# Attention scores in two matmul passes: the low part of the keys gets a zero-padded 128-row tile per head

## The chip, the cores and the metric

The kernel runs on one core of a Trainium2 chip. Five engines work side by side, each through its own queue in order: TensorE (matmuls; PE in the profile, its weight loads are shown apart as PEld), VectorE (DVE), ScalarE (ACT), GpSimd (POOL) and SyncE (SP), which issues the DMA transfers. The metric is the time of one execution on the device, in microseconds; lower is better.

## The reference, cut to what matters

The program is a two-layer block with three branches (mLSTM, sparse attention, retention) and a feed-forward part, for 512 tokens of width 1024. The change touches the attention branch alone. Its logits are, for 8 heads of width 64:

```python
q = (c_q @ a_wuq).reshape(b, s, A_HEADS, A_HEAD_DIM)
q_lat = einsum('bshd,hdc->bshc', q, a_wuk) * A_HEAD_DIM ** -0.5
logits = einsum('bthc,btkc->bthk', q_lat, kv_sel)
logits = where(valid, logits + bias, -inf)
probs = softmax(logits, axis=-1)
out = einsum('bthk,btkc->bthc', probs, kv_sel)
```

The 128 keys of a query are chosen by an indexer beforehand; the kernel keeps all keys and adds a mask instead. It moves `a_wuk` to the other side of the product: it computes a key of 64 numbers for each head and token from `c_kv`, and multiplies the query of 64 numbers with that.

## The kernel before

**Precision.** Large products are made of two parts per operand: a high part, which is the value rounded to the matmul's type by a copy, and a low part, which is the difference (`split`, lines 301 to 303: the copy on ScalarE, the subtraction on VectorE). A product is then three matmuls (`mm3`, lines 249 to 253): high by high, high by low, low by high.

**The score product.** A head is only 64 wide, and a matmul contracts over up to 128 rows of its operands. So `q_pair` (line 592) stores the query of a head twice in one 128-row tile: the high part in 64 rows, the low part in the other 64 (even heads have the high part in rows 0 to 63, odd heads in rows 64 to 127). `prepare` (line 671) makes the keys for a pair of heads: the tile `kk` of a head has the high part of its key in both halves. The first pass of line 707, `qs` by `kk` over 128 rows, is therefore (high + low query) by high key. What is left is high query by low key. The low parts of both heads of a pair lie in one tile, `kl`, the even head's in rows 0 to 63 and the odd head's in rows 64 to 127; the second pass of line 707 takes the 64 rows of a head from `qs` and from `kl`. Both passes add up in one PSUM tile.

**Units.** A unit (line 699) is one head and one block of 128 queries, 8 x 4 = 32 per layer. It makes the two score passes over 256, 256, 384 or 512 keys, adds bias and mask (`cmb`, GpSimd, line 709), adds that to the scores and takes the maximum (`prob`, `amx`, VectorE, line 712), exponentiates (ScalarE, line 715), transposes the probabilities (TensorE, line 721), copies them (ScalarE, line 723) and multiplies with the values (line 728). After a head's last block ScalarE scales the four results (`ha`, line 734).

**Order.** The units are generators. `wave_lazy` advances all that are under way by one step for each new one, and `tick` feeds them into the projections of the other branches (lines 558 to 565), one step for every two feature blocks or token blocks of a weight chunk. So a few short attention matmuls stand between runs of 512-column projection matmuls (`mm3`, lines 251 to 253). The order of each engine is fixed when the program is built; an engine waits in place when its next instruction isn't ready.

**Buffers.** Most tiles of 512 columns come from one pool, tag `r`, with 28 buffers (`NR`, line 142) that are handed out in turn: a new tile's first write waits until the last reader of the tile that had its buffer is done. `kk`, `kl`, `qs`, `cmb`, `prob` and `probT` are all of that tag.

**A twin.** The indexer (lines 623 and 624) has a product of the same build: `qs` with high and low query as weights, twice, by the high and the low part of its keys, both over 128 rows.

Of the kernel before, what the change touches and what calls it, by code (L numbers as in the profile page):

```python
# [11 lines left out]
F32 = mybir.dt.float32  # L12
F32R = mybir.dt.float32r
# [75 lines left out]
def wave_lazy(gens):  # L89
    active = []  # L90
    for g in gens:
        active.append(g)
        for x in list(active):
            if next(x, active) is active:
                active.remove(x)
        yield
    while active:
        for x in list(active):
            if next(x, active) is active:
                active.remove(x)  # L100
        yield


class Block:
# [546 lines left out]
    def attention(self, l, CT, masks, haT):  # L651
        nc, a = self.nc, self.a
        kv = [x[:, 3, :] for x in CT]
        V = [self.r(f"vv{s}") for s in range(NT)]
        with self.tc.high_priority():
            raw = self.wp.tile([128, 8, 64], F32, name="wuv", tag="raw", bufs=2)
            hi = self.wp.tile([128, 512], F32R, name="uvh", tag="whi")
            lo = self.wp.tile([128, 512], F32R, name="uvl", tag="wlo")
            nc.sync.dma_start(raw, a["a_wuv"][l].rearrange("h c d -> c h d"))
            self.split(hi, lo, raw.rearrange("p h d -> p (h d)"))  # L660
        for s in range(NT):
            p = self.sm()
            self.mm3(p, [x[:, s * 128:(s + 1) * 128] for x in kv], [hi, lo], True, True)
            nc.scalar.activation(V[s], p, AF.Copy)
            yield
        uk = self.r("uk", [4, 128])
        nc.sync.dma_start(uk, a["a_wuk"][l].rearrange("(f s) d c -> (s d) f c", s=2))
        ha = [self.r(f"ha{t}") for t in range(NT)]
        heads = {}

        def prepare(h):
            if h % 2 == 0:
                f = h // 2
                W = self.chunk(0, 2, [(0, a["a_wuq"][l][:, f * 128:(f + 1) * 128])], 128)
                p = self.sm()[:, 0:128]
                nc.tensor.transpose(p, uk[:, f, :], self.ident)
                ut = self.r("ut", [2, 128], F32R)
                self.split(ut[:, 0], ut[:, 1], p)
                qs = self.q_pair(W, 0, CT, 0.125, 0)
                yield  # L680
                p = self.sm()
                self.mm3(p, [ut[:, v] for v in range(2)], kv, True, True)
                kk = [self.r(f"kk{s}", dtype=F32R) for s in range(2)]
                lo = self.r("kl", dtype=F32R)
                for s in range(2):
                    x, y = (slice(0, 64), slice(64, 128))[::1 - 2 * s]
                    self.split(kk[s][x], lo[x], p[x])
                    nc.scalar.activation(kk[s][y], p[x], AF.Copy)
                heads["pair"] = qs, kk, lo
            qs, kk, lo = heads["pair"]  # L690
            tb = self.wk.tile([128, T], F32, name="tb", tag="tb", bufs=2)
            src = self.bias_dram[h, 0, 127:128]
            nc.sync.dma_start(tb, bass.AP(tensor=src.tensor, offset=src.offset, ap=[[639, 128], [1, T]]))
            s = h % 2
            x = slice(64 * s, 64 * s + 64)
            heads[h] = (qs[s], qs[s][x]), (kk[s], lo[x]), tb
            yield

        def unit(h, b):
            if b == 0:  # L700
                heads[h] += (self.sm([128, NT, 64]), self.stat(NT, "asum"))
            q, kk, tb, o, sums = heads[h]
            S = 128 * (b + 1)
            SP = max(S, 256)
            p = self.sm()[:, 0:SP]
            for v in range(2):
                nc.tensor.matmul(p, lhsT=q[v][:, b * 128:(b + 1) * 128], rhs=kk[v][:, 0:SP], start=v == 0, stop=v == 1)  # L707
            c = self.r("cmb", [S])
            nc.gpsimd.tensor_add(c, tb[:, T - S:T], masks[b] if b else self.neg)  # L709
            P = self.r("prob", [S])  # L710
            mx = self.stat(1, "amx")
            nc.vector.tensor_tensor_reduce(P, p[:, 0:S], c, 1.0, -3.0e38, op0=OP.add, op1=OP.max, accum_out=mx)  # L712
            nm = self.stat(1, "anm")
            nc.vector.tensor_scalar(nm, mx, -1.0, None, op0=OP.mult)
            nc.scalar.activation(P, P, AF.Exp, bias=nm, accum_out=sums[:, b:b + 1])
            yield
            yield
            yield
            pt = self.sm([128, 4, 128])
            for s in range(b + 1):  # L720
                nc.tensor.transpose(pt[:, s, :], P[:, s * 128:(s + 1) * 128], self.ident)  # L721
            PT = self.r("probT", [b + 1, 128])
            nc.scalar.activation(PT, pt[:, 0:b + 1], AF.Copy)
            yield
            yield
            yield
            for s in range(b + 1):
                nc.tensor.matmul(o[:, b, :], lhsT=PT[:, s, :], rhs=V[s][:, h * 64:(h + 1) * 64],  # L728
                                 start=s == 0, stop=s == b)
            if b == NT - 1:  # L730
                ri = self.stat(NT, "ari")
                nc.vector.reciprocal(ri, sums)
                for t in range(NT):
                    nc.scalar.activation(ha[t][:, h * 64:(h + 1) * 64], o[:, t, :], AF.Copy, scale=ri[:, t:t + 1])

        def units():
            yield prepare(0)
            yield iter(())
            for h in range(8):
                for b in range(NT):  # L740
                    if b == 2.0 and h < 7:
                        yield prepare(h + 1)
                    yield unit(h, b)

        yield from wave_lazy(units())
        for v, x in enumerate(self.branch_T("haT")):
            haT[v] = x
        for b in range(NT):
            self.to_T(ha[b].rearrange("p (f d) -> p f d", f=4), haT, b)
            yield  # L750
# [272 lines left out]
```

## Time and profile before

| | |
|---|---|
| median of 3 runs | 1861.61 us (1861.01 to 1861.81) |
| span of the profiled execution | 1862.3 us |
| TensorE busy | 1829.2 us (98%) |
| VectorE busy | 984.3 us (53%) |
| ScalarE busy | 734.4 us (39%) |
| GpSimd busy | 207.4 us (11%) |

The profiled execution is one execution; the median comes from others without the profiler, and the span counts from the first to the last instruction. A row of a timeline gives the start in us, the length in us, the engine, the line, the operation, what it writes and from what, and the form; `128*128 128x512` is a matmul that contracts over 128 rows into 128 rows of output, 512 columns wide, and `64*128` one over 64 rows. "xN" is a count, and a bracket at the end the idle time of the engine before it and what ended it. Matmuls overlap in their pipeline, so that a matmul's length is longer than its share of the engine: what a matmul costs is read from its start to the start of the next. A row of a table by stretch gives the stretch, its length, the busy time and the number of instructions of each engine in the order PE, PEld, DVE, ACT, POOL, then the granted clock of TensorE (1.00 is 2.4 GHz, 0.50 is 1.2 GHz), the busy share of the DMA engines and GB/s. In a group by line the numbers after the bar are the busy time in us, the mean in ns of one instruction, and the idle time before them with what ended it.

### The profile page before, as it was taken

To read this page: it belongs to the slowest core of one execution; us is meant where nothing else is said; L and a number is where in the kernel's file an instruction comes from. 1 tells how busy PE (TensorE), PEld (TensorE's weight loads), DVE (VectorE), ACT (ScalarE), POOL (GpSimd) and SP (SyncE) were. 2 spreads that over 40 slices of the span, in tenths; PEclk is the share of its full clock that TensorE was granted. 3 is DMA by queue.
4 is the path that set the end of the run, shared out by engine and by line. 5 is a ranking of instruction groups with operands and counts; after the bars stand their busy time and mean duration, and the time that the engine had idled before them with its cause. 6 is when DMAs were issued, how large, how long until landed. Compare 5 with 4: busy or idle time off the path is not lost.

```text
span 1862.3 us, 22844 instructions
## 1 busy us (share of the span) xinstructions
PE 1829.2 (98%) x8720; PEld 1504.7 (81%) x8720; DVE 984.3 (53%) x1798; ACT 734.4 (39%) x1202; POOL 207.4 (11%) x258
## 2 busy tenths in 40 slices
PE   9989999999999999999999899999999999999998
PEld 7868887777888888888888688877788898888886
DVE  5788985355455333332358899744545453333223
ACT  5552235555424323321245523355554343232221
POOL 3112240121000000000020132301210000000000
PEclk9989999999999999999999899999999999999999
DMA  5622323223234332323242223232222353323222
GB/s 183 204 79 74 111 72 100 79 71 97 80 136 136 102 100 92 102 91 102 100 128 80 62 80 102 66 105 82 72 74 95 109 164 97 101 92 102 91 99 82
DMA packets 126845, 185.95 MB, mean 100 GB/s; under 512 B 12256, under 2 KB 71136, under 8 KB 126736
## 3 DMA queue, kind: packets, MB, share of 16 engines
q1 hardware_dynamic: 125408, 178.98, 30.2%
q0 software_dynamic: 1184, 5.26, 0.8%
q8 instruction: 68, 1.11, 0.2%
q14 instruction: 41, 0.34, 0.1%
q10 hardware_dynamic: 144, 0.26, 0.1%
HBM read 177.64 MB, written 6.84 MB: 99 GB/s over the span
## 4 chain that ended last, share of the span: by engine, by line
PE 57%; DVE 8%; DMA 1%; issue 1%; ACT 1%; POOL 1%; SPq 0%; POOLq 0%; ACTq 0%; DVEq 0%
PE mm L251 18%; PE mm L253 18%; PE mm L252 17%; DVE wlo L234 2%; DVE mask L647 1%; PE sm L707 1%; DVE top L646 1%; PE sm L728 1%; DMA raw<-w_up 1%; PE sm L721 0%; POOL lnr L308 0%; ACT whi L233 0%; DVE ru L521 0%; DVE bst L356 0%; PE sm L345 0%
## 5 line engine op out<-in xcount | busy, mean ns | idle before, releaser
L234 DVE TENSOR_TENSOR wlo<-raw,whi 128x1024 fp32r<-128x1024 f32 (+2 forms) x302 | 371.7, 1232 | 598.0 <-ACT whi L233 597.5
L233 ACT ACTIVATE whi<-raw 128x1024 fp32r<-128x1024 f32 (+2 forms) x302 | 314.0, 1040 | 737.5 <-PE mm L252 303.6
L251 PE MATMUL mm<-hT,whi 128*128 128x512 f32 (+1 forms) x1216 | 469.3, 386 | 0.9 <-ACT fg L956 0.9
L252 PE MATMUL mm<-hT,whi 128*128 128x512 f32 (+1 forms) x1216 | 460.9, 379 | 1.0 <-DVE hT L303 1.0
L253 PE MATMUL mm<-hT,wlo 128*128 128x512 f32 (+1 forms) x1216 | 461.1, 379 | 0.0
L251 PEld LDWEIGHTS mm<-hT,whi 128*128 128x128 f32 x1216 | 228.8, 188 | 48.0 <-issue 4.6
L253 PEld LDWEIGHTS mm<-hT,wlo 128*128 128x128 f32 x1216 | 228.7, 188 | 44.0 <-issue 0.4
L252 PEld LDWEIGHTS mm<-hT,whi 128*128 128x128 f32 x1216 | 229.0, 188 | 42.1 <-DVE hT L303 1.6
L251 PE MATMUL mm<-whi,hT 128*128 128x512 f32 (+1 forms) x448 | 178.7, 400 | 1.7 <-ACT hT L302 1.7
L253 PE MATMUL mm<-whi,hT 128*128 128x512 f32 (+1 forms) x448 | 178.1, 398 | 0.0
L252 PE MATMUL mm<-wlo,hT 128*128 128x512 f32 (+1 forms) x448 | 177.4, 396 | 0.0
L253 PEld LDWEIGHTS mm<-whi,hT 128*128 128x128 f32 x448 | 86.0, 192 | 18.1 <-issue 0.9
L251 PEld LDWEIGHTS mm<-whi,hT 128*128 128x128 f32 x448 | 86.0, 192 | 17.6 <-ACT hT L302 2.1
L252 PEld LDWEIGHTS mm<-wlo,hT 128*128 128x128 f32 x448 | 86.1, 192 | 17.3 <-issue 1.3
L709 POOL TENSOR_TENSOR cmb<-tb,mask 128x256 f32<-128x256 f32 (+2 forms) x48 | 52.2, 1090 | 247.0 <-PE sm L721 78.7
L253 PE MATMUL mm<-whi,fa 128*128 128x512 f32 x192 | 75.6, 394 | 0.0
L251 PE MATMUL mm<-whi,fa 128*128 128x512 f32 x192 | 75.5, 393 | 0.0
L252 PE MATMUL mm<-wlo,fa 128*128 128x512 f32 x192 | 75.5, 393 | 0.0
L320 POOL TENSOR_SCALAR rs<-ms 128x1 f32<-128x1 f32 x16 | 5.7, 355 | 622.0 <-ACT hn L318 622.0
L712 DVE CUSTOM_DVE_ANT_0 prob<-sm,cmb 128x128 f32<-128x128 f32 (+1 forms) x64 | 31.1, 488 | 64.1 <-PE sm L707 63.4
L251 PE MATMUL mm<-whi,fr 128*128 128x512 f32 x160 | 62.4, 390 | 0.0
L253 PE MATMUL mm<-whi,fr 128*128 128x512 f32 x160 | 62.3, 389 | 0.0
(284 smaller groups left out, 2689.7 us busy)
## 6 DMA issues: line engine op xcount, KB each, us to landing
raw<-w_in SPq DMA_DIRECT2D x104, 512.0 KB, 3.5
raw<-w_gate SPq DMA_DIRECT2D x96, 256.0 KB, 2.8
raw<-w_up SPq DMA_DIRECT2D x96, 256.0 KB, 3.1
raw<-w_down SPq DMA_DIRECT2D x44, 512.0 KB, 3.6
raw<-w_out SPq DMA_DIRECT2D x16, 512.0 KB, 3.6
x<-x SPq DMA_DIRECT2D x8, 512.0 KB, 5.9
rot<-c_rot SPq DMA_DIRECT2D x16, 256.0 KB, 2.7
tb<-bias_dram SPq DMA_DIRECT2D x16, 256.0 KB, 3.4
```

Source lines behind the costliest of these rows:

```text
L233: nc.scalar.activation(h, r, AF.Copy)
L234: nc.vector.tensor_sub(o, r, h.bitcast(F32))
L251: t.matmul(out, lhsT=A[0], rhs=B[0], start=start, stop=False)
L252: t.matmul(out, lhsT=A[0], rhs=B[1], start=False, stop=False)
L253: t.matmul(out, lhsT=A[1], rhs=B[0], start=False, stop=stop)
L320: nc.gpsimd.tensor_scalar(r, ms[:, 0:1], ms[:, 1:2], EPS, op0=OP.add, op1=OP.add)
L646: nc.vector.max(m8, acc)
L647: nc.vector.match_replace(acc, m8, acc, TAKEN)
L707: nc.tensor.matmul(p, lhsT=q[v][:, b * 128:(b + 1) * 128], rhs=kk[v][:, 0:SP], start=v == 0, stop=v == 1)
L709: nc.gpsimd.tensor_add(c, tb[:, T - S:T], masks[b] if b else self.neg)
L712: nc.vector.tensor_tensor_reduce(P, p[:, 0:S], c, 1.0, -3.0e38, op0=OP.add, op1=OP.max, accum_out=mx)
L728: nc.tensor.matmul(o[:, b, :], lhsT=PT[:, s, :], rhs=V[s][:, h * 64:(h + 1) * 64], start=s == 0, stop=s == b)
```

## The change

Each head of a pair gets its own low tile, `kl0` and `kl1`, with the low part of its key in the rows in which its query has the high part. The other 64 rows are set to zero by a memset on GpSimd. The second pass takes all 128 rows of `qs` and of that tile; the rows in which the query has its low part meet the zeros.

```diff
--- before.py
+++ after.py
@@ -681,19 +681,19 @@
                 p = self.sm()
                 self.mm3(p, [ut[:, v] for v in range(2)], kv, True, True)
                 kk = [self.r(f"kk{s}", dtype=F32R) for s in range(2)]
-                lo = self.r("kl", dtype=F32R)
+                kl = [self.r(f"kl{s}", dtype=F32R) for s in range(2)]
                 for s in range(2):
                     x, y = (slice(0, 64), slice(64, 128))[::1 - 2 * s]
-                    self.split(kk[s][x], lo[x], p[x])
+                    nc.gpsimd.memset(kl[s][y].bitcast(F32), 0.0)
+                    self.split(kk[s][x], kl[s][x], p[x])
                     nc.scalar.activation(kk[s][y], p[x], AF.Copy)
-                heads["pair"] = qs, kk, lo
-            qs, kk, lo = heads["pair"]
+                heads["pair"] = qs, kk, kl
+            qs, kk, kl = heads["pair"]
             tb = self.wk.tile([128, T], F32, name="tb", tag="tb", bufs=2)
             src = self.bias_dram[h, 0, 127:128]
             nc.sync.dma_start(tb, bass.AP(tensor=src.tensor, offset=src.offset, ap=[[639, 128], [1, T]]))
             s = h % 2
-            x = slice(64 * s, 64 * s + 64)
-            heads[h] = (qs[s], qs[s][x]), (kk[s], lo[x]), tb
+            heads[h] = (qs[s], qs[s]), (kk[s], kl[s]), tb
             yield
 
         def unit(h, b):
```

The order of TensorE is the same row for row, but for the names and heights of these operands. Two things differ on other engines. In the rows below a bracket names the semaphores that an instruction waits for, by the engine or the DMA queue that raises them.

GpSimd, where the units of the fourth and fifth head stand (first layer; the names in it are `cmb`, bias plus mask of a unit, from `tb`, the bias, and a mask, and the `kl` tiles of the third pair). Before:

```order
L709 TENSOR_TENSOR cmb_3328<-tb_3199,mask1_434 128x256 [waits PE_49,Activation_49]
L709 TENSOR_TENSOR cmb_3433<-tb_3199,mask2_435 128x384 [waits DVE_49,PE_49,Activation_49]
L709 TENSOR_TENSOR cmb_3464<-tb_3199,mask3_436 128x512 [waits DMAHW1_49,PE_49]
L709 TENSOR_TENSOR cmb_3505<-tb_3428,cm_81 128x128 [waits DMAHW0_49,PE_49]
L709 TENSOR_TENSOR cmb_3535<-tb_3428,mask1_434 128x256 [waits DVE_49]
```

and in the changed kernel:

```order
L709 TENSOR_TENSOR cmb_3334<-tb_3205,mask1_434 128x256 [waits PE_49,Activation_49]
L687 MEMSET kl0_3427 64x512 [waits PE_49,Activation_49,Pool_49]
L687 MEMSET kl1_3428 64x512 [waits DVE_49,PE_49]
L709 TENSOR_TENSOR cmb_3442<-tb_3205,mask2_435 128x384 [waits PE_49,Pool_49]
L709 TENSOR_TENSOR cmb_3473<-tb_3205,mask3_436 128x512 [waits PE_49]
L709 TENSOR_TENSOR cmb_3514<-tb_3437,cm_81 128x128 [waits DMAHW0_49,DVE_49]
L709 TENSOR_TENSOR cmb_3544<-tb_3437,mask1_434 128x256 [waits PE_49,Activation_49]
```

Two memsets have come in ahead of the `cmb` of the fourth head's third block, and they wait for readers of the buffers that they get. All tiles after them get other buffers than before, so that the `cmb` of the fifth head's first block (`cmb_3505`, now `cmb_3514`) waits for VectorE instead of TensorE.

ScalarE, in the same place (`kk1` is the odd head's key tile of the third pair, `prob` the scores of the fourth head's third and fourth block, `anm` their negated maximum). Before:

```order
L723 ACTIVATE probT_3459<-sm_3456 128x256 [waits PE_49]
L688 ACTIVATE kk1_3420<-sm_3415 64x512 [waits DVE_49]
L715 ACT_TABLE_LOAD
L715 ACTIVATE prob_3435,asum_3288<-prob_3435,anm_3438 128x384 [waits DVE_49]
L715 ACTIVATE prob_3466,asum_3288<-prob_3466,anm_3469 128x512 [waits DVE_49,PE_49]
```

and in the changed kernel:

```order
L723 ACTIVATE probT_3468<-sm_3465 128x256 [waits PE_49]
L689 ACTIVATE kk1_3426<-sm_3421 64x512 [waits DVE_49]
L715 ACT_TABLE_LOAD [waits DVE_49]
L715 ACTIVATE prob_3444,asum_3294<-prob_3444,anm_3447 128x384 [waits Activation_49]
L715 ACTIVATE prob_3475,asum_3294<-prob_3475,anm_3478 128x512 [waits DVE_49,PE_49]
```

The load of the exponential's table stood free of waits; now it carries the wait for VectorE, and the exponential behind it, which waited for VectorE, waits for ScalarE's own earlier reader of a buffer.

## Rows read from the trace of the kernel before

**Rows 1.** Page, part 1: busy time, share of the span, instructions, TensorE alone

```profile
PE 1829.2 (98%) x8720; PEld 1504.7 (81%) x8720; DVE 984.3 (53%) x1798; ACT 734.4 (39%) x1202; POOL 207.4 (11%) x258
```

**Rows 2.** Table by stretch, first layer's attention stretch: busy time by engine

```profile
306.70:462.60 155.90, 154.77 (x737) 121.87 (x737) 74.91 (x170) 90.39 (x184) 27.05 (x27) 0.99 0.26 82
```

**Rows 3.** Line 707, its low pass: duration ns, starts, forms with counts

```profile
L707 PE MATMUL sm<-kl,qs x64: 379/410/502, 307.1 to 1383.8; 64*128 64x256 f32 x32, 64*128 64x384 f32 x16, 64*128 64x512 f32 x16
```

**Rows 4.** Timeline, 307.4 to 308.9: start us, length us, engine, line

```profile
307.49 0.19 PEld L707 LDWEIGHTS sm<-kk,qs 128*128 128x128 f32 x1
...
307.72 0.28 PE L707 MATMUL sm<-kk,qs 128*128 128x256 f32 x1
...
307.92 0.18 PEld L707 LDWEIGHTS sm<-kl,qs 64*128 64x128 f32 x1 [0.25 <-issue]
307.93 0.38 PE L707 MATMUL sm<-kl,qs 64*128 64x256 f32 x1
...
308.23 0.50 PE L251 MATMUL mm<-hT,whi 128*128 128x512 f32 x1
...
308.57 0.39 PE L252 MATMUL mm<-hT,whi 128*128 128x512 f32 x1
...
308.80 0.40 PE L253 MATMUL mm<-hT,wlo 128*128 128x512 f32 x1
```

**Rows 5.** Timeline of TensorE, the indexer's two 128-row passes

```profile
63.14 0.28 PE L623 MATMUL sm<-CT,qs 128*128 128x256 f32 x1
63.26 0.28 PE L624 MATMUL sm<-CT,qs 128*128 128x256 f32 x1
63.38 0.34 PE L623 MATMUL sm<-CT,qs 128*128 128x384 f32 x1
```

**Rows 6.** Timeline of TensorE, a 512-column score pair

```profile
343.68 0.40 PE L707 MATMUL sm<-kk,qs 128*128 128x512 f32 x1
344.00 0.50 PE L707 MATMUL sm<-kl,qs 64*128 64x512 f32 x1
344.43 0.39 PE L707 MATMUL sm<-kk,qs 128*128 128x256 f32 x1
```

**Rows 7.** Groups by line of GpSimd, the memset of that shape

```profile
L425 POOL MEMSET qz<- 64x512 f32 x8 | 4.2, 520 | 5.7 <-issue 5.4
```

**Rows 8.** Timeline, all engines, 386.0 to 392.6, fourth and fifth head

```profile
386.16 1.45 POOL L709 TENSOR_TENSOR cmb<-tb,cm 128x128 f32<-128x128 f32 x1
...
388.53 0.08 DVE L712 DVE_READ_ACCUMULATOR2_ANT amx<- 128x1 f32 x1
...
388.66 1.28 ACT L715 ACT_TABLE_LOAD   x1
...
389.13 0.15 DVE L714 TENSOR_SCALAR anm<-amx 128x1 f32<-128x1 f32 x1
...
389.80 0.29 DVE L712 CUSTOM_DVE_ANT_0 prob<-sm,cmb 128x128 f32<-128x128 f32 x1
...
389.96 0.62 ACT L715 ACTIVATE prob<-prob,anm 128x384 f32<-128x384 f32 x1
...
391.60 0.50 PE L721 MATMUL sm<-cm,prob 128*128 128x128 f32 x3
...
392.37 0.39 ACT L715 ACTIVATE prob<-prob,anm 128x128 f32<-128x128 f32 x1
```

**Rows 9.** Table by stretch, granted clock: third number from the right

```profile
138.20:377.00 238.80, 235.00 (x1205) 194.10 (x1203) 172.02 (x425) 100.73 (x179) 54.09 (x55) 1.00 0.29 88
377.04:380.45 3.41, 3.41 (x9) 2.71 (x9) 2.45 (x4) 3.37 (x6) 0.00 (x0) 0.50 0.28 105
1298.64:1302.05 3.41, 3.41 (x8) 2.66 (x9) 2.35 (x4) 3.37 (x6) 0.00 (x0) 0.50 0.24 91
```

**Rows 10.** Waits of TensorE: total us, times, longest us

```profile
PE sm L915 <- DVE rsc L900: 2.9, 2, 1.4
...
PE sm L707 <- ACT ha L734: 2.0, 2, 1.0
```

## Prediction

> **What bounds the kernel now.** I read the page's first part first: TensorE is busy for 98% of the span [rows 1]. That share alone proves little, because a matmul's row counts as busy until its modelled end, so I read starts instead of lengths from here on. The second view is the table of one stretch, the 156 us of the first layer in which the attention units are fed into the projections. TensorE is busy for 154.77 of 155.90 us there, ScalarE for 90.39, VectorE for 74.91, GpSimd for 27.05 [rows 2]. The second layer repeats it, up to its last low pass at 1383.8 [rows 3]. So in the place that the change touches TensorE sets the pace, and time taken out of its queue is time off the end, unless another engine's answer then comes too late.
>
> The third view is the group of the low pass: 64 matmuls of form 64*128, 32 of them 256 columns wide, 16 of 384 and 16 of 512 [rows 3]. The fourth is TensorE's timeline, read from start to start. A 512-column projection matmul starts 0.23 us before the next one (308.57 to 308.80). Around a low pass all three steps are longer [rows 4]. The high pass of 256 columns starts at 307.72, the low pass at 307.93 (0.21 later), the next projection matmul at 308.23 (0.30 later), and the one after it at 308.57 (0.34 instead of 0.23). The weight loads say why: the high pass's load starts at 307.49, 0.23 us ahead of its matmul, while the low pass's starts at 307.92, together with it. The matmul ahead of a 64-row one takes longer, the 64-row one has its load in the open, and so has the one behind it.
>
> **What the change takes away.** The kernel before has a twin of the new form: the indexer's two passes (lines 623 and 624), both over 128 rows, with the same weights loaded twice as in line 707. Their 256-column steps are 0.12 and 0.12 us (63.14, 63.26, 63.38) [rows 5]. So a 256-column pair with the step behind it takes 0.21 + 0.30 + 0.34 = 0.85 us now, and as 128-row matmuls 0.12 + 0.12 + 0.23 = 0.47: 0.38 us less. For 512 columns the pair starts at 343.68, the low pass at 344.00 and the next matmul at 344.43, thus 0.32 + 0.43 = 0.75 us against 2 x 0.23 = 0.46 [rows 6]; with the same 0.11 of the step behind, 0.40 less. I take 0.39 for 384 columns, which lies between. The sum is 32 x 0.38 + 16 x 0.39 + 16 x 0.40 = 24.8 us. Both row halves are in these 64, and TensorE's order is the same row for row in the changed kernel, so nothing is added on that engine.
>
> The Trainium skill has a rule for this ("TensorEngine Tiling (Array Packing)", Key Properties): changing the tiling mode drains the engine. The trace agrees in kind [rows 4]. With the 128 cycles that "TensorE: Matmul & The Clock Gate", Step-by-step: what each phase is for, gives for a drain, two per pair at 2.4 GHz are an estimate of 64 x 0.107 = 6.8 us, a quarter of what the steps show; the steps decide, since they hold the loads too.
>
> **What it adds.** Sixteen GpSimd memsets of 64 x 512, two per pair of heads, four pairs per layer. The same shape takes 0.52 us where the program has it already [rows 7], so 16 x 0.52 = 8.3 us of GpSimd, which is busy for 27 of 156 us there [rows 2]. They are not free by themselves: GpSimd works in order, a memset waits until the last reader of its buffer is done, and behind it stand the additions of bias and mask (cmb, line 709), for which VectorE's prob (line 712) waits. I went through the waits that the changed order names and set each releaser's end in the trace against the waiter. The second low tile also moves which buffer every later tile of the 28 gets. The closest case is the cmb of the fifth head's first block. It starts at 386.16 now and will wait for amx of an earlier unit, written until 388.61; its 1.45 us then end at 390.06, and the prob that reads it starts at 389.80 [rows 8]. That prob comes 0.3 us late, and VectorE's order now puts a gate multiply (line 493) ahead of it as well. What waits for it first is ScalarE's exponential, which starts at 392.37, 2.3 us after that prob ends at 390.09 [rows 8]; this cover hides it and I cost it at nothing. Were the cover gone, TensorE would lose the 0.3 us in each layer. The memsets themselves I also cost at nothing: their tiles are read a head later.
>
> **What comes late next.** TensorE gets ahead of answers that it waits for. The closest one in the order is ScalarE's table load ahead of the exponential of the fourth head's third block. It runs at 388.66 now, before VectorE's anm at 389.13 is there; in the changed order the load itself waits for anm, which ends at 389.28. So the exponential ends at 389.28 + 1.28 + 0.62 = 391.2 instead of 390.58, and its transposes (line 721) start at 391.60 now [rows 8]. Two score pairs stand on TensorE's way there, 0.78 us, so about 0.6 + 0.78 - 1.0 = 0.4 us is waited, in each layer. Other answers come close where short matmuls stand in a row; I allow 0.35 us more per layer, so 1.5 us in all. The bounds are nothing (no wait is removed, so no gain) and three places per layer that each lose two pairs' saving, 2 x 3 x 0.78 = 4.7 us. I take 1.5, near the one place that I can work out.
>
> The clock is the last term. TensorE's granted clock was 0.50 in 377.04 to 380.45 and in 1298.64 to 1302.05, behind the two idles of 1.0 us of line 707, and 1.00 from 138.20 to 377.00, though that stretch has one of the two idles of 1.4 us of line 915 [rows 9, 10]. So a short idle does not bring it down by itself; what lies around it decides. At 0.50, the 1.2 GHz level, 3.41 us hold 8 matmuls of 0.43 instead of 15 of 0.23, a loss of about 1.6 us each. In the changed kernel all of this comes some us earlier and closer together, so I take the more common outcome of such an idle, that both falls are gone: 3.2 us.
>
> **The sum.** The profiled execution's span is 1862.3 us: 1862.3 - 24.8 + 1.5 - 3.2 = 1835.8. The median of the runs before, 1861.6, is 0.7 below that span, so I forecast 1835.1 us.
>
> **The rivals.** (1) The gain comes as worked out, but the clock falls in these places again, or in others: 1835.1 + 3.2 = 1838.3 us. For it speaks that both layers fell at the same place. (2) TensorE gets ahead of softmax everywhere: score pass, prob, exponential and transposes of a unit hang together, and half of the saving turns into waits: 1862.3 - 12.4 - 0.7 = 1849.2. Against it stands ScalarE's share of 90 in 156 us [rows 2]. (3) The 128-row form gains nothing: a full-height load cannot start while a full-height matmul runs, both loads of a pair stay in the open, and the steps stay 0.21, 0.30, 0.34: 1861.6 us. Against it stand the load at 307.49, ahead of its matmul, and the twin's 0.12 [rows 4, 5]. The Trainium skill states it so ("TensorE: Matmul & The Clock Gate", The mechanism): a load overlaps a running matmul only where the row groups differ; the trace differs. (4) Slower: the memsets stand ahead of the cmb additions, and their buffers come free so late that VectorE, and then TensorE in its fixed order, waits once in each of the 8 pairs for a whole lead of cmb over prob, 389.80 - 386.16 = 3.64 us [rows 8]. It decides from the point where 8 such waits exceed 24.8 us, that is 3.1 us each; 8 x 3.64 = 29.1, so 1861.6 + 4.3 = 1865.9. Against it stands that the releasers found end a head before the use.
>
> **How the numbers follow.** Forecast 0.50, rival 1 0.28, rival 2 0.12, rival 3 0.03, rival 4 0.03, and 0.04 for a larger gain. A measurement of this kernel can tell some 0.2%, 3.7 us, from no change: forecast, rivals 1 and 2 and the larger gain are faster (0.94), rival 3 is the same (0.03), rival 4 slower (0.03). The range goes down to 1831.8 (no waits: 1833.6; one half-clock stretch fewer elsewhere: 1.6 more, plus the error of steps read to 0.01 us) and up to 1841.5 (rival 1 with the waits at their bound, 3.2 more). Beyond it lie rivals 2 to 4 and half of the 0.04, 0.20 together.
>
> **What would show it.** In the profile after, the second pass of line 707 (708 there) should have the form 128*128, its load should start about 0.2 us ahead of it, and the steps of a 256-column pair should be 0.12, 0.12, 0.23. The attention stretch should shrink by about 12 us in each layer, and everything before 306 us stay. Waits of TensorE for prob or cmb at that place would be rivals 2 or 4. Steps still at 0.30 would be rival 3 and the prediction's end. Granted clock of 0.50 inside the stretch would be rival 1.

## The result, and the profile after

| | before | after |
|---|---|---|
| median, same chip | 1861.31 us (1859.96 to 1861.81, 4 runs) | 1838.68 us (1837.55 to 1840.39, 4 runs) |
| span of the profiled execution | 1862.3 us | 1838.5 us |
| attention stretch, layer 1 / layer 2 | 166.5 / 166.7 us | 154.2 / 154.3 us |
| the rest, up to the end of TensorE's last matmul | 1521.5 us | 1522.6 us |

The ratio is 0.9888 with an interval of 0.9877 to 0.9899; the medians are 22.6 us apart. Of 1861.31 us the interval is 18.8 to 22.9 us, so a saving is known to some 2 us, and no closer. The forecast was 1835.1 us, range 1831.8 to 1841.5. The attention stretch is counted here from the first start of line 707 in a layer to the start of TensorE's 59th row behind the last one, on the same instructions in every kernel.

First the page of the kernel after, part 1, and a table by stretch (stretch, its length, busy time of PE, PEld, DVE, ACT, POOL, granted clock, DMA share, GB/s). They answer [rows 1, 2, 9].

```profile
PE 1803.9 (98%) x8720; PEld 1497.9 (81%) x8720; DVE 985.8 (54%) x1798; ACT 733.1 (40%) x1202; POOL 215.1 (12%) x274
...
306.40:460.90 154.50, 152.62 (x797) 128.28 (x797) 78.33 (x176) 93.99 (x194) 29.91 (x33) 1.00 0.29 88
1216.40:1370.90 154.50, 152.60 (x796) 128.13 (x796) 78.31 (x176) 93.83 (x194) 29.91 (x33) 1.00 0.28 84
```

TensorE is busy for 98% as before, with as many instructions; the busy share alone would not tell that anything had happened. The granted clock is 1.00 over both attention stretches, where one fall of 3.41 us made 0.99 of it in [rows 2]; the falls at 377 and 1298 us [rows 9] are not there. GpSimd has 16 instructions and 7.7 us more.

Next the group of the low pass (length ns least/median/most, first and last start, forms) and TensorE's timeline around one 256-column pair, as in [rows 3, 4].

```profile
L707 PE MATMUL sm<-kl,qs x64: 274/310/401, 306.8 to 1360.1; 128*128 128x256 f32 x32, 128*128 128x384 f32 x16, 128*128 128x512 f32 x16
```

```profile
306.92 0.40 PE L253 MATMUL mm<-hT,wlo 128*128 128x512 f32 x1
306.92 0.19 PEld L707 LDWEIGHTS sm<-kk,qs 128*128 128x128 f32 x1
307.15 0.28 PE L707 MATMUL sm<-kk,qs 128*128 128x256 f32 x1
307.16 0.19 PEld L707 LDWEIGHTS sm<-kl,qs 128*128 128x128 f32 x1
...
307.27 0.28 PE L707 MATMUL sm<-kl,qs 128*128 128x256 f32 x1
307.27 0.19 PEld L251 LDWEIGHTS mm<-hT,whi 128*128 128x128 f32 x1
307.39 0.40 PE L251 MATMUL mm<-hT,whi 128*128 128x512 f32 x1
307.39 0.19 PEld L252 LDWEIGHTS mm<-hT,whi 128*128 128x128 f32 x1
```

The pair starts at 307.15 and 307.27 and the projection matmul follows at 307.39: 0.12 and 0.12 us where [rows 4] had 0.21 and 0.30. The load of the low pass starts at 307.16, 0.11 ahead of its matmul; before it started with it. Medians of the steps in ns, each over the places where the neighbours on that side are projection matmuls and nothing waits:

| columns of the pair | step of the high pass | step of the low pass | step behind (512 columns) |
|---|---|---|---|
| 256 | 209 → 117 | 310 → 119 | 337 → 233 |
| 384 | 264 → 173 | 370 → 174 | 337 → 233 |
| 512 | 327 → 231 | 431 → 234 | 337 → 233 |

Most high passes stand behind a transpose (line 721) or a product with the values (line 728); their step is some 0.08 us longer in both kernels and falls by the same 88 to 96 ns. So a 64-row low pass cost 0.09 us ahead of it, 0.19 in itself (0.20 at 384 and 512 columns) and 0.10 behind.

### The profile page after: what moved, and what is told of

Same layout as the page of the kernel before. It is cut to its first block, busy times and chain, and to the rows that moved or that the text cites. A ratio compares the mean times of both kernels' runs of the same rounds, so it can differ in the third digit from the quotient of the medians.

```text
span 1838.5 us, 22889 instructions
## 1 busy us (share of the span) xinstructions
PE 1803.9 (98%) x8720; PEld 1497.9 (81%) x8720; DVE 985.8 (54%) x1798; ACT 733.1 (40%) x1202; POOL 215.1 (12%) x274
## 4 chain that ended last, share of the span: by engine, by line
PE 58%; DVE 7%; DMA 1%; ACT 1%; issue 1%; POOL 1%; SPq 0%; POOLq 0%; ACTq 0%; DVEq 0%
PE mm L253 18%; PE mm L251 18%; PE mm L252 18%; DVE wlo L234 2%; DVE mask L647 1%; DVE top L646 1%; PE sm L728 1%; DMA raw<-w_up 1%; PE sm L707 1%; ACT whi L233 1%; PE sm L721 0%; DVE ru L521 0%; PE sm L368 0%; POOL lnr L308 0%; PE sm L345 0%
## 5 line engine op out<-in xcount | busy, mean ns | idle before, releaser
L252 PE MATMUL mm<-wlo,fr 128*128 128x512 f32 x160 | 62.3, 389 | 0.0
```

The source lines that it names most:

```text
L252: t.matmul(out, lhsT=A[0], rhs=B[1], start=False, stop=False)
```

## What the experiments had to tell apart

The theory: the price belongs to the change of matmul height, 128 rows to 64 and back, and is paid on each visit; the zeros, memsets and other buffers are free or nearly so; what of the gain is missing went into a few waits on softmax. The rivals: the gain came by the other buffers or the clock and not by the height; each 64-row matmul is dear by itself; the memsets or the wait at the table load took a share back. Times of the kernel before that stand beside a run are from the same chip. That the zeros themselves make the second pass fast is not among the rivals: the twin of [rows 5] has the same step of 0.12 us with both halves full.

**The changed kernel once more.** It shows how much one execution differs from the next.

> The changed kernel again, beside the others on one chip. Both theories: 22 to 24 us under the kernel before, TensorE waiting 0.6 us per layer for the exponential at 384 us.

Measured: 1838.51 us (1838.21 to 1840.99) against 1860.23 for before, ratio 0.9881 (0.9868 to 0.9895). The stretches are 154.18 and 154.33 us. The rest is 2.2 us shorter than in the first profile, with 3.4 us less of half clock around 1034 us. So a stretch repeats within 0.1 us, and differences of 2 us in the rest of two profiles say nothing.

**All of the change but the height.** The two padded tiles, the memsets and the new buffers stay; the second pass takes 64 rows again.

```diff
-            heads[h] = (qs[s], qs[s]), (kk[s], kl[s]), tb
+            x = slice(64 * s, 64 * s + 64)
+            heads[h] = (qs[s], qs[s][x]), (kk[s], kl[s][x]), tb
```

> The changed kernel's tiles and memsets, but the low pass takes 64 rows again (the zeros are never read). Theory (the height of the matmul is what costs): steps back at 0.21, 0.30, 0.34 us, time within 2 us of the kernel before, so 1860 to 1863. Rival (two heads no longer share one low tile, and that is what frees TensorE): near 1839.

Measured: 1861.39 us against 1860.23, ratio 1.0006 (0.9997 to 1.0015). The group of the low pass (line 708 in this kernel) and TensorE's timeline:

```profile
L708 PE MATMUL sm<-kl,qs x64: 379/410/502, 308.0 to 1381.8; 64*128 64x256 f32 x32, 64*128 64x384 f32 x16, 64*128 64x512 f32 x16
```

```profile
308.62 0.28 PE L708 MATMUL sm<-kk,qs 128*128 128x256 f32 x1
308.83 0.38 PE L708 MATMUL sm<-kl,qs 64*128 64x256 f32 x1
309.14 0.50 PE L251 MATMUL mm<-hT,whi 128*128 128x512 f32 x1
309.47 0.40 PE L252 MATMUL mm<-hT,whi 128*128 128x512 f32 x1
```

The steps are 0.21, 0.31 and 0.33 again. The whole gain hangs on the height: the interval of the ratio leaves room for at most 0.6 us of it. The stretches are 166.65 us, with one fall of the clock in it, and 165.36 without: the memsets and the buffers cost nothing that shows, and a fall of 3.41 us at half clock costs some 1.3 us.

**Half of the heads.** Even heads with 128 rows, odd heads with the 64 rows that hold their key.

```diff
-            heads[h] = (qs[s], qs[s]), (kk[s], kl[s]), tb
+            x = slice(64, 128) if s else slice(0, 128)
+            heads[h] = (qs[s], qs[s][x]), (kk[s], kl[s][x]), tb
```

> Even heads take the low pass over 128 rows, odd heads over 64. Theory (a fixed price per low pass of 64 rows between matmuls of 128): half the steps fall, the two attention stretches shrink by about 6.2 us each, time about 11 to 12 us under the kernel before. Rival (the price is paid once per stretch or depends on which half of the rows): nearly all or nearly none of the gain.

Measured: 1848.48 us against 1859.31, ratio 0.9938 (0.9923 to 0.9953). The stretches are 159.07 and 159.42 us, about half way between 154.2 and the 165.4 of 64 rows without a fall. The price is one per low pass; it does not depend on what the other heads do.

**Two 64-row matmuls in a row.** In the kernel before, the low pass of 512 columns is cut into two of 256, with the same weights. A price per matmul would be paid twice, a price per change of height once.

```diff
-                nc.tensor.matmul(p, lhsT=q[v][:, b * 128:(b + 1) * 128], rhs=kk[v][:, 0:SP], start=v == 0, stop=v == 1)
+                for c0, c1 in ((0, 256), (256, 512)) if v and SP == 512 else ((0, SP),):
+                    nc.tensor.matmul(p[:, c0:c1], lhsT=q[v][:, b * 128:(b + 1) * 128], rhs=kk[v][:, c0:c1],
+                                     start=v == 0, stop=v == 1 and c1 == SP)
```

> The kernel before with the 512-column low pass cut into two 64-row matmuls of 256 columns with the same weights; 16 matmuls more. Theory A (the price is in the change of height): the step from the first half to the second is 0.12 us, that from the second to the next 0.30 as before. Theory B (every 64-row matmul has its load in the open): 0.30 for both halves, 0.18 x 16 = 3 us more in all.

Measured: 1859.94 us in one run, against 1859.31. TensorE and its weight loads at such a place; "x2" are the two halves in one row:

```profile
343.99 0.40 PE L708 MATMUL sm<-kk,qs 128*128 128x512 f32 x1
...
344.32 0.29 PEld L708 LDWEIGHTS sm<-kl,qs 64*128 64x128 f32 x2 [0.36 <-issue]
344.32 0.50 PE L708 MATMUL sm<-kl,qs 64*128 64x256 f32 x2
...
344.75 0.39 PE L708 MATMUL sm<-kk,qs 128*128 128x256 f32 x1
```

From the first half at 344.32 to the next pass at 344.75 it is 0.43 us, as for the uncut pass in [rows 6]. The medians of the two steps are 223 and 207 ns, 430 in all against 431, and the step behind is still 337. The expected split, 0.12 and 0.30, did not come. The first half's load starts 2 ns ahead of its matmul, the second's 116 ns ahead: it overlaps the first half, which takes the same 64 rows. So a visit of two 64-row matmuls pays once. How the sum splits tells more: against the 119 ns of 256 columns without a change, the first half has 0.10 more and the second 0.09. These are the price behind a change and the price ahead of one, so the 0.19 of a single low pass is the first change's second part and the second change's first part.

The same cut with 128 rows is the control.

> The same cut in the changed kernel, as a control: two 128-row halves of 256 columns. Both theories: 0.12 us for each half, no difference to the changed kernel in the sum.

Measured: 1838.54 us in one run; halves of 118 and 119 ns, 237 against 234 uncut. The cut itself is free.

**The low pass first.** In the kernel before, the 64-row pass goes ahead of the 128-row one.

```diff
-            for v in range(2):
-                nc.tensor.matmul(p, lhsT=q[v][:, b * 128:(b + 1) * 128], rhs=kk[v][:, 0:SP], start=v == 0, stop=v == 1)
+            for v in (1, 0):
+                nc.tensor.matmul(p, lhsT=q[v][:, b * 128:(b + 1) * 128], rhs=kk[v][:, 0:SP], start=v == 1, stop=v == 0)
```

> The kernel before with the two passes of line 707 in the other order, the 64-row low pass first. Theory (a change of height in the middle of 128-row matmuls has a price on both sides, whatever stands there): the low pass keeps its 0.30, 0.37 and 0.43 us, the step of the matmul behind it, now the high pass, is about 0.1 longer, and the step ahead of it too; the attention stretches as in the kernel before, 165 to 167 us. Rival (the price comes from two passes into one PSUM tile in this order): it changes by more than 3 us per stretch.

Measured: 1859.0 us in one run, against 1859.66. TensorE:

```profile
307.35 0.39 PE L253 MATMUL mm<-hT,wlo 128*128 128x512 f32 x1
307.67 0.38 PE L707 MATMUL sm<-kl,qs 64*128 64x256 f32 x1
307.98 0.38 PE L707 MATMUL sm<-kk,qs 128*128 128x256 f32 x1
308.20 0.40 PE L251 MATMUL mm<-hT,whi 128*128 128x512 f32 x1
```

Now the projection matmul ahead takes 0.32 instead of 0.23, the low pass 0.31, and the high pass behind it 0.22 instead of 0.12. The three parts of the price have moved with the 64-row matmul. The stretches are 164.50 us and, with one fall of the clock, 166.10. No order within the pair avoids it.

**The memsets away.** Three low tiles outside the pool, zeroed once; the pool has 26 buffers instead of 28 for the room.

```diff
-NB8, NR = 8, 28
+NB8, NR = 8, 26
...
-                kl = [self.r(f"kl{s}", dtype=F32R) for s in range(2)]
+                kl = [self.low[0], self.low[1 + f % 2]]
...
-                    nc.gpsimd.memset(kl[s][y].bitcast(F32), 0.0)
```

> The changed kernel without memsets in the loop: three low tiles stand outside the pool and are zeroed once in each half that stays zero, with 26 buffers of tag r (the same memory as 29). Theory (GpSimd's memsets are hidden): within 1 us of the run with 29 buffers, unless the other buffers bring waits of their own. Rival (the 16 memsets cost VectorE or TensorE something): 3 us or more under it.

Measured: 1839.62 us against 1860.23, ratio 0.9882 (0.9869 to 0.9896), the same as the changed kernel. The memsets were hidden. The stretches are 0.3 to 0.5 us shorter, and the wait of line 721 that comes below is not in this kernel's waits.

**One more buffer.** With 29 buffers the table load of the exponential stands free of its wait again.

```diff
-NB8, NR = 8, 28
+NB8, NR = 8, 29
```

> The changed kernel with 29 instead of 28 buffers of tag r. Theory (the waits that ate part of the gain come from the buffers having moved by one, which put a wait on ScalarE's table loads): the table loads stand free again, TensorE's waits at 384, 418 and 431 us go, 2 to 3 us per execution less than the changed kernel, about 25 to 26 us under the kernel before. Rival (TensorE now simply outruns softmax): the waits stay, within 1 us of the changed kernel.

Measured: 1838.49 us against 1860.23, ratio 0.9877 (0.9862 to 0.9892). The stretches are 153.25 and 153.46 us, 0.8 to 0.9 less per layer, and the wait of line 721 is gone. The load of the table, which waits for `anm` in the changed kernel, here follows the activation ahead of it without a wait:

```profile
385.24 0.59 ACT L689 ACTIVATE kk<-sm 64x512 fp32r<-64x512 f32 x1 [1.72 <-DVE kl L303]
385.86 1.28 ACT L715 ACT_TABLE_LOAD   x1
```

The median is that of the changed kernel, 21.7 us under the kernel before and not the 25 to 26 that were expected; an interval of some 2.8 us to either side could hardly show the 1.7 us of the stretches. In the profile there are waits elsewhere. TensorE's waits (total us, times, longest), and a table by stretch:

```profile
PE sm L915 <- DVE rsc L900: 3.5, 2, 2.9
...
PE mm L251 <- DVE sg L481: 2.2, 2, 1.1
```

```profile
252.93:256.34 3.41, 3.41 (x18) 3.41 (x17) 1.86 (x9) 0.60 (x1) 0.23 (x1) 0.50 0.34 88
```

Line 251 now waits for `sg`, 1.1 us in each layer, which is more than the stretch gained; the profiles of the changed kernel have no such wait. Line 915 waits once for 2.9, and 3.41 us at half clock stand behind that; this may belong to this execution alone, which was the longest of the four (1841.62). That the table load's wait came with the buffers is shown; that the wait for `sg` is what kept the median where it was is likely, but one profile does not show it.

**The same edit on other short matmuls.** The mLSTM's gate rows are products over 36 rows (lines 800 and 811, 12 matmuls). Here they are padded to 128 with zeros, on top of the change.

```diff
-        self.sel = self.const.tile([36, 4], F32R, name="sel")
+        self.sel = self.const.tile([128, 4], F32R, name="sel")
...
-        rows = [self.r("rows", parts=36, dtype=F32R) for _ in range(2)]
+        rows = [self.r("rows", dtype=F32R) for _ in range(2)]
...
```

> The changed kernel with the mLSTM's 12 matmuls of 36 rows (lines 800 and 811) padded to 128 rows in the same way, since their rows show steps of 0.33 us for 512 columns at full clock and up to 0.72 at half clock. Theory (a matmul of fewer rows costs the same here): the steps around them fall to 0.23 (0.43 at half clock); 1 to 3 us under the changed kernel unless TensorE's wait of 3.6 us for VectorE just ahead takes it up, then nothing. Rival (only 64-row forms cost): steps unchanged.

Measured: 1832.47 us against 1859.31, ratio 0.9852 (0.9836 to 0.9869), about 6 us below the changed kernel (1838.54 in the control on the same chip), more than expected. TensorE in the changed kernel, at half clock:

```profile
131.66 0.63 PE L252 MATMUL mm<-wlo,hT 128*128 128x512 f32 x1
132.21 0.79 PE L800 MATMUL sm<-rows,sel 36*128 36x512 f32 x1
132.94 0.79 PE L253 MATMUL mm<-whi,hT 128*128 128x512 f32 x1
133.53 0.63 PE L251 MATMUL mm<-whi,hT 128*128 128x512 f32 x1
```

and with 128 rows:

```profile
131.51 0.63 PE L252 MATMUL mm<-wlo,hT 128*128 128x512 f32 x1
131.94 0.63 PE L800 MATMUL sm<-rows,sel 128*128 128x512 f32 x1
132.36 0.63 PE L253 MATMUL mm<-whi,hT 128*128 128x512 f32 x1
132.79 0.63 PE L251 MATMUL mm<-whi,hT 128*128 128x512 f32 x1
```

The three steps go from 0.55, 0.73 and 0.59 to 0.43, 0.42 and 0.43. Over the 12 matmuls the longer steps add up to some 3 us. The rest of the gain comes along with less half clock: the half-clock stretches around these places are 6.8 and 3.4 us long, in the padded kernel of the next run 3.4 and 6.8, so 10.2 us in both; in the ten profiles without the padding they add up to 20.5 to 23.9. So this is not one execution's chance. How much of the 6 us that made is not split further here, and why the stretches are shorter is not shown.

**Both.** The padded gate rows and the tiles zeroed once.

> The kernel with padded 36-row operands of the mLSTM, and the low tiles outside the pool as in the run without memsets. Theory (both effects add up): 0.5 to 1.5 us under the run with padded 36-row operands, 1831 to 1832, TensorE's wait for the exponential in the fourth head gone. Rival (the other 26 buffers bring waits elsewhere, as the 29 did): the same as that run or above it.

Measured: 1830.24 us (1828.84 to 1832.24, 5 runs) against 1859.66, ratio 0.9841 (0.9827 to 0.9854). It beats the kernel before and the changed one; its interval overlaps that of the padded gate rows alone, so that the tiles add something there is not shown.

## Where the prediction was right, and where not

**Steps: right.** Forecast 24.8 us, from the twin's 0.12 [rows 5]. The measured steps give 32 x 0.387 + 16 x 0.391 + 16 x 0.397 = 25.0, and putting the 64 rows back gives it all up. The second pass is still in line 707 (the prediction wrote 708), its form is 128*128, and its load starts 0.12 us ahead at 256 columns, not 0.2. The stretch of a layer shrank by 12.4 us; the forecast said about 12. That this is also nearly what the steps alone give, 12.5, is luck: the fall of the clock that went and the waits that came cancel, as worked out below. The rule that a load overlaps a running matmul only where the row groups differ (the Trainium skill, "TensorE: Matmul & The Clock Gate", The mechanism), the ground of rival 3, does not hold for the loads here: 128-row loads run 0.11 us ahead of a 128-row pair's second matmul, and a 64-row load 116 ns ahead behind a 64-row matmul of the same rows; the same section excepts loads into a background weight buffer, and no run here shows which buffer a load takes.

**Memsets at nothing: right.** They cost no time with the 64 rows back, and leaving them out brought nothing. The `cmb` of the fifth head waited for `amx` as read from the order (below, 381.71), but it took 0.46 us and not the 1.45 that the prediction carried over, so it ended at 382.17, well ahead of the `prob` that reads it (383.48). The 0.3 us that the prediction gave to that `prob` did not arise.

**The wait at the table load: the right place, 0.8 us instead of 0.4.** The kernel after, fourth head, to set beside [rows 8]:

```profile
381.55 0.08 DVE L712 DVE_READ_ACCUMULATOR2_ANT amx<- 128x1 f32 x1
381.55 0.69 DVE L493 TENSOR_TENSOR sg<-mm,sg 128x512 f32<-128x512 f32 x1
...
381.71 0.46 POOL L709 TENSOR_TENSOR cmb<-tb,cm 128x128 f32<-128x128 f32 x1 [2.48 <-DVE amx L712]
...
382.15 0.14 DVE L714 TENSOR_SCALAR anm<-amx 128x1 f32<-128x1 f32 x1
...
382.38 1.28 ACT L715 ACT_TABLE_LOAD   x1 [0.71 <-DVE anm L714]
...
383.46 0.33 PE L728 MATMUL sm<-vv,probT 128*128 128x64 f32 x2
383.48 0.28 DVE L712 CUSTOM_DVE_ANT_0 prob<-sm,cmb 128x128 f32<-128x128 f32 x1
...
383.67 0.61 ACT L715 ACTIVATE prob<-prob,anm 128x384 f32<-128x384 f32 x1
...
384.44 0.55 PE L721 MATMUL sm<-cm,prob 128*128 128x128 f32 x3 [0.64 <-ACT prob L715]
```

and TensorE at the same place in the kernel before:

```profile
391.44 0.33 PE L728 MATMUL sm<-vv,probT 128*128 128x64 f32 x2
391.60 0.50 PE L721 MATMUL sm<-cm,prob 128*128 128x128 f32 x3
```

ScalarE idles 0.71 us until `anm` is there, then loads the table, then exponentiates. TensorE's idle time counts 0.64 us, but from line 728 to line 721 it takes 0.98 us instead of 0.16, so the wait costs 0.8. The forecast's sum had TensorE come 0.78 us nearer to `anm`; from `anm` to line 728 it is 1.31 us (382.15 to 383.46) where it was 2.31 (389.13 to 391.44), so it came 1.0 nearer. VectorE's multiply of line 493, which takes 0.69, sits between `amx` and `anm`. The waits of TensorE for the whole program:

```profile
PE sm L707 <- ACT ha L734: 2.0, 2, 1.0
...
PE sm L721 <- ACT prob L715: 1.3, 2, 0.6
```

Line 721's row is new; that of line 707 is as in [rows 10].

**The other waits: too small.** I allowed 0.35 us per layer. TensorE's order is the same row for row, so the two profiles can be compared step by step. In a layer's stretch the dearer steps give 12.5 us and the rows at half clock 1.2; the stretch shrank by 12.4. So 1.4 us per layer (1.36) are waited away, 2.7 in all instead of 1.5. Of these 0.8 are line 721's, and some 0.6 lie around 418 and 431 us, where score pairs and short matmuls stand with few projections between. After, and below it before:

```profile
417.69 0.28 PE L707 MATMUL sm<-kl,qs 128*128 128x256 f32 x1
...
417.99 0.74 PEld L728 LDWEIGHTS sm<-vv,probT 128*128 128x128 f32 x6 [0.23 <-ACT probT L723]
418.00 0.88 PE L728 MATMUL sm<-vv,probT 128*128 128x64 f32 x6
```

```profile
427.75 0.38 PE L707 MATMUL sm<-kl,qs 64*128 64x256 f32 x1
428.06 0.88 PE L728 MATMUL sm<-vv,probT 128*128 128x64 f32 x6
```

The step of that low pass is 0.31 us as before, where it is 0.12 elsewhere: the product behind it waits for `probT` of line 723.

**The clock: mis-sized, and the larger error.** That both falls would go was right: none of the 14 layer stretches profiled with 128 rows in all low passes has one. But I took 3.2 us off for it. First, a fall cost about 1.2 to 1.6 us (1.2 in the rows of the kernel before; the two layers of the kernel with the 64 rows put back differ by 1.3, those of the one with the low pass first by 1.6). Second, and more, the profile from which I took two falls is not what the median holds: of the 8 layer stretches of four kernels with 64 rows throughout, 4 have a fall. The profile of before was itself a long execution: its span is 1862.3 us, while the 31 executions of the same kernel beside the experiments have median spans of 1857.8 (24 with a mean granted clock of 0.993 or more) and 1860.2 (7 with 0.992 or less); its own clock is 0.990. The recorded time of an execution is its span plus 1.8 to 1.9 us, and I read "0.7 below the span" off two different executions as if it were an offset. So that 0.7 had already brought the sum from a long execution to the median, and the 3.2 took off falls that the median's executions had at most in part.

The account of the two profiles: 25.0 for the steps, 2.5 for two falls, less 2.7 of waits, less 1.0 in the rest (where profiles differ by 2 us anyway) is 23.8, as the spans differ. The account of the medians: 25.0 less 2.7 is 22.3, and 0.3 is left for the falls that the runs of before had, where the forecast had 3.2. So the forecast was 3.6 us too low: 1.2 by the waits and 2.9 by the clock, less 0.3 by which the kernel before was faster beside this run (1861.31 instead of 1861.61) and 0.2 more that the steps saved. The clock's share is what is left over, and the medians are not known to better than some 2 us, so it is an account and not a measurement. Each of these terms lies within the bounds that were given, and the range held.

**The rivals.** Rival 1's 1838.3 is the nearest number, but its mechanism, falls of the clock in the stretch, did not happen; the clock is 1.00 there. Rival 2 (half the saving lost) is 2.7 of 25 instead. The sign that was named for it and for rival 4, a wait of TensorE for `prob` at that place, did appear; but the forecast had such a wait in its own sum, so the sign could not tell them apart, and only its size does. Rivals 3 and 4 fell with the steps and the memsets.

## What to carry to other kernels

Look in the timeline for matmuls over fewer rows than their neighbours and compare the start-to-start steps of the one ahead, of itself and of the one behind with those of a full-height matmul of the same width; if the weight load starts with its matmul, the price of the change of height is in the open, and zero rows can cost less than it, as here, where GpSimd had time for the memsets. Collect short-height matmuls into one run if they can't be padded, since a run of two pays once. And take a term for the granted clock from several executions: one profile shows a fall, or doesn't, by chance.

## What was not expected of the hardware

Each change of matmul height, down or up, cost 0.19 us: 0.09 in the step of the matmul ahead of it and 0.10 in the step of the one behind it, at 256, 384 and 512 columns, and in whichever order the passes stood. A visit to 64 rows is two changes, 0.39 us. It is there for 36 rows too: at full clock the steps around the two matmuls of line 811 are 327, 335 and 324 ns where they are 235, 233 and 237 with the padding, and at half clock, around those of line 800, the matmul ahead of the change has 0.13 more and the one behind it 0.17 (558 and 594 ns against 427; 555 and 593 on the way back). The matmul ahead, which has full height itself, pays a part of the price. A single change of the number of buffers, from 28 to 29, moved 0.9 us of waiting out of each attention stretch, and in the one profile taken line 251 waited 1.1 us in each layer at a place where it had not waited.
